# A two-layer hybrid backbone on one core: order of query and value projections, placement of query transposes, first fill, sums of squares, and buffers of the second layer's gate

## The chip, the cores and the metric

The kernel runs on one core of one Trainium2 chip. The metric is the device time of one execution in microseconds. Kernels are compared by the median of their runs; beside it one execution of each kernel is profiled.

## The reference

Two layers work on 512 latent tokens (an 8 x 64 grid) and 256 context tokens of width 1024, all in float32. A layer is:

- a modulation vector from `silu(c) @ ada_w` for latent tokens and `silu(c_ctx) @ ada_w` for context tokens (shift, scale and gate, twice);
- a modulated RMS norm and one input projection, whose columns go to three head groups: a Fourier mixer (256 columns), neighbourhood attention (6 heads of 64, with RMS norm of queries and keys, a relative position bias and a window of 8 x 16; latent queries also see all context keys), and gated linear attention (4 heads, key width 48, value width 96, chunks of 64, one scan per direction, latent scans beginning from the context's final state);
- the concatenated results through one output projection, gated and added to the stream;
- a second modulated RMS norm and a SwiGLU feed-forward network (2816 hidden columns), gated and added.

```python
y = jnp.concatenate([y_fn, y_na, y_gla], axis=-1) @ w_out
x = x + g_m * y
x = x + g_f * swiglu(ada_modulate(x, norm_ffn, sh_f, sc_f), ffn_w1, ffn_w3, ffn_w2)
```

The context stream is updated in the first layer only; the second layer needs its keys, values and states, and no context queries. The output is the latent stream.

## The kernel before, in words

**Precision.** A large product is made of three (`mm3`, line 183): each operand is split into a rounded part and a remainder (`split`, 197: a ScalarE copy and a subtraction on VectorE or GpSimd), and high x high, low x high and high x low are added in PSUM. All these matmuls carry line 181, so the trace is read by tile names: `u` is an unnamed tile, `whl` a split weight, `raw` its load, `a`, `b`, `m`, `y` the four kinds of PSUM buffers (3, 2, 2 and 1 of them, one bank each).

**Order.** Instructions are traced in program order; a list planner with a timeline of its own then orders each engine, except where the block is marked `manual_schedule` for PE (attention, output projection, norm), where PE keeps the written order. All loads and stores are issued by SyncE's queue, one behind the other. An issue waits in that queue for its data, or for the space that it writes. `issue_after(last_mm[0])` keeps PE's instructions of the block behind the last matmul traced so far.

**A layer's stages.** (1) Norm and the input projection, in groups of columns (`group`, 560), one tile of 128 tokens after another: linear-attention values, their queries and keys, gates, then the attention's keys (`wg` 2), values (3) and queries (4). Keys and queries go through a head norm (`headnorm`, 704: a ScalarE square, a VectorE reduction, a GpSimd power, two VectorE products), values through one ScalarE copy; all three are stored to a scratch tensor in HBM (732), to be read back in another order. In layer 0 each tile also takes two steps of `ada_steps` (260), in which VectorE multiplies columns of the modulation weights and PE collects them. Linear attention runs in between: `gate(i)`, `decays(i)` and `kvstate(i)` come 2, 4 and 6 ticks behind tile i (622 to 624). They use the pads `glp` and `kend` and the exponentials `ab`, each in two buffers.

(2) After the Fourier projection the scratch is read back (`load_heads`, 879: keys, then queries; biases; values), the linear-attention outputs are transposed (`to_features`), and the Fourier transform runs as a generator (`fourier`, 1032), whose steps are the weights, the features of each tile of 128 columns, and the two products with the DFT tables. After 6 of its steps (layer 1: 3), `stacks_of_heads` (908) transposes keys and queries of the first pair of heads on PE (924), and splits them into the stacks `st`.

(3) Attention runs over units of a pair of heads and a block of columns (`Heads`, 1150; 5 blocks per pair in layer 0, 4 in layer 1): scores of unit n, transposes of the probabilities of unit n - 1, a fill, and the values of unit n - 1. The fill is work of the output projection's first part (`wo`, over the linear-attention and Fourier features, 5 x 128 rows): a credit in us is raised by 2.4 (layer 1: 2.3) per unit, and products are issued while it is positive:

```python
credit[0] += us
while credit[0] > 0:
    n = next(wo, None)
    if n is None: return
    credit[0] -= n[1] * 3 / 2400
```

The credit begins at -2.4 (1137). What is left of `wo` runs after the last unit.

(4) The second part of the output projection (`wb`, over the attention features) adds into the residual stream (`u<-m,u,u`, line 192 from 994), one product per 128 rows m and stream n: context and latent in layer 0, the two halves of the latent tokens in layer 1. Behind each product `norm_add` (363) squares the new rows on ScalarE (`nsq`) and adds them to `nacc`: stream 0 on VectorE, stream 1 on GpSimd. `norm_sums` (382) sums `nacc` over partitions on PE, with a power on GpSimd; `norm_spread` (397) brings the result back to all partitions (`ndg`); `norm_mod` applies it. At the same time GpSimd splits the first feed-forward weights (1344).

(5) The feed-forward network in three parts; in layer 0 the steps of layer 1's modulation run beside it.

Of the kernel before, what the change touches and what calls it, by code (L numbers as in the profile page):

```python
# [16 lines left out]
F32 = mybir.dt.float32  # L17
F32R = mybir.dt.float32r
U32 = mybir.dt.uint32
AF = mybir.ActivationFunctionType  # L20
ALU = mybir.AluOpType
# [4 lines left out]
KD = 8  # L26
# [116 lines left out]
def hybrid_kernel(tc, d, out, dbg=None):  # L143
    nc = tc.nc
    ctx = ExitStack()
    V, S, G, T = nc.vector, nc.scalar, nc.gpsimd, nc.tensor
# [9 lines left out]
    def mk(p, shape, dt=F32, tag=None, bufs=None):  # L156
        uid[0] += 1
        kw = {}
        if bufs:
            kw["bufs"] = bufs  # L160
        return p.tile(shape, dt, tag=tag or f"u{uid[0]}", name=f"{tag or 'u'}_{uid[0]}", **kw)
# [6 lines left out]
    PA = lambda: mk(psp, [128, 512], F32, "a", 3)  # L168
# [9 lines left out]
    last_mm = [None]  # L178
# [9 lines left out]
    def tt(e, o, a, b, op):  # L188
        e.tensor_tensor(out=o, in0=a, in1=b, op=op)  # L189
# [4 lines left out]
    def act(o, i, f=AF.Identity, **kw):  # L194
        S.activation(out=o, in_=i, func=f, **kw)  # L195
# [164 lines left out]

        return products, finish

    def norm_add(acc, x, k, tp, e):

        if k == 0:
            act(acc, x, AF.Square)
            return
        sq = mk(tp, [128, TL], F32, "nsq", 2)[:, :x.shape[-1]]
        act(sq, x, AF.Square)
        tt(e, acc, acc, sq, ALU.add)  # L370

    def norm_acc(xs, n, tp, e):

# [77 lines left out]
    for l in range(DEPTH):  # L451
        last = l == DEPTH - 1
        ctx_q = not last
# [11 lines left out]
        np0 = pool(nst_, f"n{l}", "left")  # L465
# [81 lines left out]
        tp = pool(p1, f"t{l}", "right")  # L547
# [8 lines left out]
        s1p = pool(s1, f"gs{l}", "left")  # L556
# [3 lines left out]
        def group(src, cols, specs, evac, together=0, w=None, ps=None, after=None):  # L560

            w = w or wgroup(src, cols)
            ps = ps or {}
            for n, (i, c0) in enumerate(specs):
                if n == len(specs) - together:
                    for m, (j, cj) in enumerate(specs[n:]):
                        ps[j] = dense("mbmbya")[:, :cols - cj]  # L570
                    for k in range(KD):
                        for j, cj in specs[n:]:
                            token_major(ps[j], w, j, cj, k)
                if i not in ps:
                    ps[i] = dense("mb" if l == 0 else "mbmby")[:, :cols - c0]
                    for k in range(KD):
                        token_major(ps[i], w, i, c0, k)
                tick()
                evac(i, ps[i])
                next(steps, None)  # L580
                next(steps, None)
                if after:
                    after()
# [42 lines left out]
        both = [(i, 0) for i in tiles]  # L626
        qonly = [(i, 0) for i in qtiles]

        npad = 2
        kend = [mk(s1p, [128, 8, 64]) for _ in range(npad)]  # L630
        glp = [mk(s1p, [128, 8, 64]) for _ in range(npad)]
        qT = {i: mk(gp, [128, 4, 128]) for i in qtiles}
# [9 lines left out]
        def gate(i):  # L642
            zps = PA()[:, :384]
            mm(zps, aT[:, 128 * i:128 * i + 128], alpha, True, True)
            ab = mk(s1p, [128, 512], F32, "ab", 2)[:, :384]
            act(ab, zps, AF.Abs)
            act(ab, ab, AF.Exp, scale=-1.0)
            act(ab, ab, AF.Ln, bias=1.0)
            stt(glp[i % npad][:, :, 0:48], v3(zps), 0.0, v3(ab), ALU.min, ALU.subtract)

        def decays(i):
            gl, ke = glp[i % npad], kend[i % npad]
            heads = lambda a, dp: a[:, 2 * dp:2 * dp + 2].rearrange("p a b -> p (a b)")
            if i not in qtiles:
                dps = PA()
                for dp in range(4):
                    mm(dps[:, 2 * dp:2 * dp + 2], heads(gl, dp), ind, dp == 0, True)
                act(dec[:, i].rearrange("p a b -> p (a b)"), dps[:, 0:8], AF.Exp, scale=1.0 / 16)
            bs = PA()[:, :384]
            for dr in range(2):  # L660
                mm(v3(bs)[:, 4 * dr:4 * dr + 4], tri[:, 2 * dr + 1], gl[:, 4 * dr:4 * dr + 4, 0:48], dr == 0, True)
            ee = mk(s1p, [128, 512], F32, "ab", 2)[:, :384]
            act(ee, bs, AF.Exp, scale=1.0 / 16)
            kb = gqk[i][:, 4:8, 0:48][:, None].to_broadcast([128, 2, 4, 48])
            tt(V, p4(ke), kb, v4(ee), ALU.mult)
            if i in qtiles:
                bi = PA()
                for dp in range(4):
                    mm(bi[:, 128 * dp:128 * dp + 128], heads(gl, dp), tri[:, dp // 2 * 2], dp == 0, True)
                raw = PA()  # L670
                for a in range(4):
                    T.transpose(raw[:, 128 * a:128 * a + 128], heads(gqk[i], a), ident)
                d3 = lambda a: a.rearrange("p (d a b) -> p d a b", d=2, a=2)
                for dst, sgn, x in ((qT[i], 1.0, raw[:, 0:256]), (kT[i], -1.0, raw[:, 256:512])):
                    eb = mk(s1p, [128, 512], F32, "ab", 2)
                    act(eb, bi, AF.Exp, scale=sgn / 16)
                    x = x.rearrange("p (a b) -> p a b", a=2)[:, None].to_broadcast([128, 2, 2, 128])
                    tt(V, dst.rearrange("p (d a) b -> p d a b", d=2), x, d3(eb), ALU.mult)
                    if sgn > 0:
                        for dr in range(2):  # L680
                            G.tensor_copy(dec[:, i, 2 * dr:2 * dr + 2],
                                          d3(eb)[:, dr, :, 63 - 63 * dr::64])
# [137 lines left out]

        group(d["wg"][l, 1], 384, qonly, ev_scr("g"))
        group(d["wg"][l, 2], 384, both, ev_scr("k"), after=between)
        group(d["wg"][l, 3], 384, both, ev_scr("v"), after=between)
        group(d["wg"][l, 4], 384, qonly, ev_scr("q"), after=between)


        ze = [mk(zp, [128, 2, 258], F32R) for _ in range(2)]
# [3 lines left out]
        for m in range(2):  # L831
            sl = slice(128 * m, 128 * m + 128)
            for (hs, n) in ((hc, TC), (hl, TL)):
                if hs is hc and not ctx_q:
                    continue
                ps = dense("mb" if l == 0 else "mbmby")[:, :n]
# [39 lines left out]
        nap = pool(yst, f"nq{l}", "right")  # L876
# [31 lines left out]
        def stacks_of_heads(p):  # L908

            for src, gain in ((kn, None), (qn, qg)):  # L910
                n = 768 if ctx_q or gain is None else 512
                kinds = (0, 1) if gain is None else (2,)
                for hh in range(2):
                    for k in kinds:
                        stacks[0, hh, k] = mk(p, [128, n], F32R, f"st{hh}{k}")
                for (j0, nj) in ((0, 4), (4, 2)):
                    if src is qn and j0 and not ctx_q:
                        continue
                    c0 = 128 * j0 if src is qn else (128 * j0 + 256) % 768
                    sl = slice(c0, c0 + 128 * nj)  # L920
                    pss = [ps()[:, :128 * nj] for ps in (PB, PA)]
                    for j in range(nj):
                        for hh, ps in enumerate(pss):
                            T.transpose(ps[:, 128 * j:128 * j + 128], src[j0 + j][:, 128 * hh:128 * hh + 128], ident)
                    for hh, ps in enumerate(pss):
                        u = [stacks[0, hh, k][:, sl] for k in kinds]
                        if gain is None:
                            split(ps, u[0], u[1])
                        else:
                            act(u[0], ps, AF.Copy, scale=gain)  # L930
                            lo = u[0][64:128]
                            stt(lo, ps[64:128], gain[64:128], lo.bitcast(F32), ALU.mult, ALU.subtract)
# [182 lines left out]
        load_heads(nap, "v", vn)  # L1115
        for _ in range(6 if ctx_q else 3):
            next(fn)
        with tc.issue_after(last_mm[0]):
            stacks_of_heads(nap)
        for _ in fn:  # L1120
            pass
        fst.close()
# [11 lines left out]

        load_streams(range(3))

        credit = [-2.4]

        def fill(us):

# [159 lines left out]
        nst_ = ExitStack()  # L1300
        np0 = pool(nst_, f"fn{l}", "left")
        accs = [mk(np0, [128, TL], F32, "nacc", 2)[:, :st_[1](0).shape[-1]] for st_ in streams]
        engines = (V, G) if ctx_q else (V, G)
        with tc.manual_schedule(engines={mybir.EngineType.PE}):
            since = 0
            for mn, _ in wb:
                if mn is None:
                    continue
                m, n = mn
                norm_add(accs[n], streams[n][1](m), m, np0, engines[n])  # L1310
                if mn == (1, 0):
                    early_w = tc.cur_priority
                if since == (1 if ctx_q else 3):
                    sums = norm_sums((accs[0], accs[0].shape[-1]), np0)
                if since == (2 if ctx_q else 7):
                    rb = norm_spread(sums, np0)
                since += bool(since) or mn == (KD - 1, 0)
# [142 lines left out]
```

## Time and profile before

| | us |
|---|---|
| median of 3 runs | 1687.62 |
| range of the runs | 1684.39 to 2008.04 |
| profiled execution | 1687.75 |
| its span | 1686.0 |
| PE busy in it | 1634.9 |
| VectorE, ScalarE, GpSimd busy | 925.9, 581.4, 236.9 |

The span runs from the first to the last instruction that the profiler shows. PE is TensorE's matmul, PEld its weight load, DVE is VectorE, ACT ScalarE, POOL GpSimd, SP or SPq SyncE's queue, whose entries are issues of transfers. `a <- b` in a list of waits reads "a waited for b"; in a row of an instruction `out<-in` names what it writes and reads. An engine that is busy all the time may still run at a lower clock: PEclk is the granted clock as a share of 2.4 GHz.

### The profile page before, as it was taken

The page shows a single profiled execution, that of the slowest core. Times are in us where ns is not written, and L with a number is a line of the kernel's source. Part 1 is how long each engine was busy: PE and PEld are TensorE (multiplying, and loading weights), DVE is VectorE, ACT ScalarE, POOL GpSimd, SP SyncE. Part 2 cuts the span into 40 slices and gives each one's busy share as a digit, 9 for nine tenths or more (in the row PEclk, how much of TensorE's full clock was granted, in tenths as well). Part 3 has the DMA queues.
Part 4 walks back from the last instruction along what each step waited for, and adds up shares of the span by engine and source line. Part 5 has one row for each costly group of instructions (what it writes and reads, how often), then busy time and mean ns, then how long its engine had stood idle before and what let it go on. Part 6 is the DMA issues. An engine that isn't in the chain of part 4 may idle for free.

```text
span 1686.0 us, 25086 instructions
## 1 busy us (share of the span) xinstructions
PE 1634.9 (97%) x9938; PEld 1415.1 (84%) x9938; DVE 925.9 (55%) x1680; ACT 581.4 (34%) x1030; POOL 236.9 (14%) x280
## 2 busy tenths in 40 slices
PE   6999999999999999999999999999899999999999
PEld 5888898787888888888888889899777888888887
DVE  6799875677755553454533443453577553344332
ACT  4474224444334311221122324832444432222220
POOL 0243331003212300000000011332102200000000
PEclk9999999999899999999999999999899999999999
DMA  9445535634133352342321311222763143223321
GB/s 339 156 153 166 185 104 170 186 91 133 41 122 124 119 186 96 126 153 85 125 63 55 120 46 40 94 91 73 202 166 111 51 138 100 95 86 107 100 86 52
DMA packets 79906, 199.68 MB, mean 118 GB/s; under 512 B 10344, under 2 KB 21164, under 8 KB 78764
## 3 DMA queue, kind: packets, MB, share of 16 engines
q1 hardware_dynamic: 79788, 198.07, 37.3%
q8 instruction: 78, 1.28, 0.3%
q14 instruction: 40, 0.33, 0.1%
HBM read 174.84 MB, written 14.29 MB: 112 GB/s over the span
## 4 chain that ended last, share of the span: by engine, by line
PE 87%; DMA 5%; DVE 3%; ACT 2%; issue 1%; SPq 1%; POOL 1%; ACTq 0%; DVEq 0%; POOLq 0%
PE a L181 29%; PE m L181 25%; PE b L181 21%; PE y L181 10%; PE b L1223 1%; DMA qn<-scr_q 1%; DVE u L192 1%; DVE whl L189 1%; DMA st<-qt 1%; DMA raw<-in_woa 1%; DMA kn<-scr_k 0%; DMA bias<-in_rpb 0%; DVE nacc L189 0%; DMA raw<-in_wg 0%; ACT ab L195 0%
## 5 line engine op out<-in xcount | busy, mean ns | idle before, releaser
L195 ACT ACTIVATE whl<-raw 128x1024 fp32r<-128x1024 f32 (+7 forms) x222 | 204.8, 928 | 386.3 <-PE a L181 140.0
L181 PE MATMUL m<-u,whl 128*128 128x512 f32 (+1 forms) x1278 | 264.8, 359 | 0.5 <-DVE whl L189 0.5
L189 DVE TENSOR_TENSOR whl<-raw,whl 128x1024 fp32r<-128x1024 f32 (+7 forms) x201 | 223.1, 1112 | 73.7 <-ACT whl L195 73.6
L181 PE MATMUL a<-u,whl 128*128 128x512 f32 (+1 forms) x1299 | 249.0, 348 | 2.9 <-ACT u L195 2.4
L181 PEld LDWEIGHTS m<-u,whl 128*128 128x128 f32 x1278 | 212.7, 192 | 33.8 <-issue 1.2
L181 PEld LDWEIGHTS a<-u,whl 128*128 128x128 f32 x1299 | 210.5, 191 | 34.4 <-ACT u L195 2.8
L181 PE MATMUL b<-u,whl 128*128 128x512 f32 (+1 forms) x915 | 184.9, 352 | 3.1 <-DVE whl L189 1.8
L181 PEld LDWEIGHTS b<-u,whl 128*128 128x128 f32 x915 | 152.2, 193 | 26.7 <-DVE whl L189 2.4
L192 DVE SCALAR_TENSOR_TENSOR adac<-adaw,u,adac 128x512 f32<-128x512 f32 x196 | 154.6, 810 | 35.9 <-DMA adaw<-in_adaw 34.5
L181 PE MATMUL b<-whl,u 128*128 128x384 f32 (+1 forms) x696 | 145.6, 344 | 1.8 <-DVE u L192 1.8
L181 PE MATMUL m<-whl,u 128*128 128x384 f32 (+2 forms) x672 | 139.7, 344 | 1.9 <-ACT u L195 1.9
L181 PEld LDWEIGHTS m<-whl,u 128*128 128x128 f32 x672 | 115.6, 188 | 16.3 <-issue 9.6
L181 PEld LDWEIGHTS b<-whl,u 128*128 128x128 f32 x696 | 121.6, 188 | 8.0 <-issue 3.3
L181 PE MATMUL a<-g,whl 128*128 128x512 f32 (+1 forms) x594 | 126.7, 370 | 0.0
L181 PEld LDWEIGHTS a<-g,whl 128*128 128x128 f32 x594 | 103.9, 189 | 19.4 <-DVE ft L192 0.8
L192 DVE SCALAR_TENSOR_TENSOR ft<-ft,a 128x512 f32<-128x512 f32 (+1 forms) x53 | 30.5, 575 | 99.7 <-ACT ft L195 65.2
L181 PE MATMUL y<-u,whl 128*128 128x512 f32 (+1 forms) x420 | 82.5, 349 | 0.1
L181 PEld LDWEIGHTS y<-u,whl 128*128 128x128 f32 x420 | 68.1, 189 | 12.1 <-issue 1.7
L181 PE MATMUL m<-g,whl 128*128 128x512 f32 (+1 forms) x396 | 77.8, 350 | 0.0
L189 POOL TENSOR_TENSOR nacc<-nacc,nsq 128x256 f32<-128x256 f32 (+1 forms) x21 | 21.0, 1002 | 391.4 <-ACT nsq L195 391.3
L181 PEld LDWEIGHTS m<-g,whl 128*128 128x128 f32 x396 | 64.7, 189 | 9.7
L181 PE MATMUL b<-g,whl 128*128 128x256 f32 (+1 forms) x396 | 72.5, 336 | 0.0
(217 smaller groups left out, 2015.2 us busy)
## 6 DMA issues: line engine op xcount, KB each, us to landing
raw<-in_w SPq DMA_DIRECT2D x104, 512.0 KB
adaw<-in_adaw SPq DMA_DIRECT2D x48, 512.0 KB
adaw<-in_adaw SPq DMA_DIRECT2D x64, 256.0 KB
raw<-in_wg SPq DMA_DIRECT2D x40, 384.0 KB
raw<-in_w SPq DMA_DIRECT2D x32, 448.0 KB
adaw<-in_ada SPq DMA_DIRECT2D x8, 1024.0 KB
st<-kt SPq DMA_DIRECT2D x32, 192.0 KB
raw<-in_woa SPq DMA_DIRECT2D x16, 320.0 KB
```

The costliest lines, as they stand in the source:

```text
L181: last_mm[0] = T.matmul(o, lhsT=l, rhs=r, start=start, stop=stop, skip_group_check=True).ins
L189: e.tensor_tensor(out=o, in0=a, in1=b, op=op)
L192: V.scalar_tensor_tensor(out=o, in0=a, scalar=s, in1=b, op0=op0, op1=op1)
L195: S.activation(out=o, in_=i, func=f, **kw)
L1223: T.transpose(ps[:, 128 * j:128 * j + 128], p[:, 128 * j:128 * j + 128], ident)
```

## The change

The group of attention queries is projected before the group of values. `stacks_of_heads` becomes a generator that stops ahead of the keys and ahead of the queries: keys are transposed where they were, then two more steps of the Fourier generator run, and the queries' transposes are kept behind the last matmul of these. The fill's credit begins at 0. For the norm ahead of the feed-forward network, one PSUM bank holds the running sums of squares of stream 0 (both layers) and of stream 1 (layer 1 only): the first square is written there, VectorE adds each later one there, and the last addition writes `nacc` in SBUF as before. Stream 1 of layer 1 so moves from GpSimd to VectorE; in layer 0 it stays on GpSimd and in SBUF. Layer 1 gets three buffers of `ab`, `kend` and `glp` in place of two.

```diff
-    def norm_add(acc, x, k, tp, e):
-
+    def norm_add(acc, x, k, tp, e, ps=None):
+
+        part = acc if ps is None else ps
         if k == 0:
-            act(acc, x, AF.Square)
+            act(part, x, AF.Square)
             return
         sq = mk(tp, [128, TL], F32, "nsq", 2)[:, :x.shape[-1]]
         act(sq, x, AF.Square)
-        tt(e, acc, acc, sq, ALU.add)
+        tt(e, acc if k == KD - 1 else part, part, sq, ALU.add)
...
-        npad = 2
+        npad = 2 + l
...
-            ab = mk(s1p, [128, 512], F32, "ab", 2)[:, :384]
+            ab = mk(s1p, [128, 512], F32, "ab", 2 + l)[:, :384]
...
-            ee = mk(s1p, [128, 512], F32, "ab", 2)[:, :384]
+            ee = mk(s1p, [128, 512], F32, "ab", 2 + l)[:, :384]
...
-                    eb = mk(s1p, [128, 512], F32, "ab", 2)
+                    eb = mk(s1p, [128, 512], F32, "ab", 2 + l)
...
         group(d["wg"][l, 2], 384, both, ev_scr("k"), after=between)
+        group(d["wg"][l, 4], 384, qonly, ev_scr("q"), after=between)
         group(d["wg"][l, 3], 384, both, ev_scr("v"), after=between)
-        group(d["wg"][l, 4], 384, qonly, ev_scr("q"), after=between)
...
             for src, gain in ((kn, None), (qn, qg)):
+                yield
                 n = 768 if ctx_q or gain is None else 512
...
+        first = stacks_of_heads(nap)
+        next(first)
         with tc.issue_after(last_mm[0]):
-            stacks_of_heads(nap)
+            next(first)
+        for _ in range(2):
+            next(fn)
+        with tc.issue_after(last_mm[0]):
+            for _ in first:
+                pass
         for _ in fn:
             pass
...
-        credit = [-2.4]
+        credit = [0.0]
...
-        engines = (V, G) if ctx_q else (V, G)
+        bank = PA()
+        sums_ps = (bank[:, 0:256], None) if ctx_q else (bank[:, 0:256], bank[:, 256:512])
...
-                norm_add(accs[n], streams[n][1](m), m, np0, engines[n])
+                norm_add(accs[n], streams[n][1](m), m, np0, V if sums_ps[n] is not None else G, sums_ps[n])
```

## Rows read from the trace of the kernel before

**Rows 1.** The profile page: engines' busy time, and the clock line of 40 slices.

```profile
PE 1634.9 (97%) x9938; PEld 1415.1 (84%) x9938; DVE 925.9 (55%) x1680; ACT 581.4 (34%) x1030; POOL 236.9 (14%) x280
...
PEclk9999999999899999999999999999899999999999
```

**Rows 2.** Waits of PE, whole run: us in total, times, longest.

```profile
PE a L181 <- DVE nacc L189: 15.7, 3, 11.5
PE a L924 <- DMA qn<-scr_q: 6.1, 5, 2.6
```

**Rows 3.** Windows: stretch, length, busy of each engine (count), PEclk, DMA share, GB/s.

```profile
192.00:228.00 36.00, 36.00 (x263) 33.47 (x262) 28.27 (x57) 8.20 (x16) 8.01 (x6) 1.00 0.55 172
281.00:313.00 32.00, 26.08 (x156) 22.30 (x154) 18.76 (x44) 14.34 (x34) 1.76 (x6) 0.84 0.62 184
403.00:433.00 30.00, 25.01 (x125) 20.21 (x124) 24.69 (x34) 11.81 (x22) 16.09 (x11) 0.92 0.35 110
433.00:442.00 9.00, 9.00 (x45) 9.00 (x45) 6.33 (x18) 2.72 (x6) 1.20 (x1) 0.51 0.35 117
1086.00:1096.00 10.00, 7.33 (x66) 5.94 (x65) 5.13 (x12) 7.41 (x13) 3.82 (x4) 1.00 0.47 140
1203.00:1229.00 26.00, 20.16 (x72) 14.89 (x72) 14.63 (x35) 10.09 (x25) 1.20 (x4) 0.61 0.58 169
1306.00:1316.00 10.00, 7.67 (x39) 7.47 (x39) 5.90 (x14) 5.96 (x11) 6.64 (x6) 0.66 0.43 143
```

**Rows 4.** Waits of PE at 281-313, layer 0.

```profile
PE a L924 <- DMA qn<-scr_q: 2.6, 2, 1.6
PE b L1223 <- DVE rcl L1201: 1.8, 1, 1.8
PE a L181 <- DVE mx L1191: 1.5, 1, 1.5
```

**Rows 5.** Waits of PE at 1186-1229, layer 1.

```profile
PE a L924 <- DMA qn<-scr_q: 3.5, 3, 2.6
PE a L181 <- DVE st L192: 1.6, 1, 1.6
PE b L1223 <- DVE rcl L1201: 1.0, 1, 1.0
```

**Rows 6.** Waits of SyncE's queue at 262-300, layer 0.

```profile
SPq L426 <- PE m L181: 5.0, 2, 4.7
```

**Rows 7.** Timeline of SyncE's queue, layer 1: start, us, what is issued.

```profile
1187.24 0.35 SPq L732 DMA_DIRECT2D scr_q<-nst  x1
1187.64 2.54 SPq L888 DMA_DIRECT2D kn<-scr_k  x4
```

**Rows 8.** VectorE by form at 228-260: count | busy, mean ns | idle before, releaser.

```profile
L709 DVE TENSOR_REDUCE hss<-hsq 128x6 f32<-128x384 f32 x6 | 3.3, 550 | 2.8 <-ACT hsq L195 2.8
...
L189 DVE TENSOR_TENSOR nst<-b,hrs 128x256 f32<-128x256 f32 x6 | 2.2, 415 | 0.3 <-POOL hrs L189 0.3
```

**Rows 9.** Timeline at the end of layer 1's attention: start, us, instruction.

```profile
1287.87 2.99 PE L181 MATMUL m<-u,whl 128*128 128x512 f32 x12
...
1289.27 0.69 DVE L1229 COPY pT<-b 128x512 f32<-128x512 f32 x1
```

**Rows 10.** VectorE by form at 403-426 (first row) and 1297-1309 (other two).

```profile
L189 DVE TENSOR_TENSOR nacc<-nacc,nsq 128x256 f32<-128x256 f32 x7 | 7.3, 1043 | 3.5 <-ACT nsq L195 3.5
...
L189 DVE TENSOR_TENSOR nacc<-nacc,nsq 128x256 f32<-128x256 f32 x7 | 6.8, 967 | 0.3 <-ACT nsq L195 0.2
...
L192 DVE SCALAR_TENSOR_TENSOR u<-b,u,u 128x256 f32<-128x256 f32 x3 | 1.4, 472 | 0.0
```

**Rows 11.** Waits of PE at 403-433, layer 0's output projection and norm.

```profile
PE b L181 <- DVE whl L189: 1.8, 2, 1.1
```

**Rows 12.** Timeline at layer 1's first sum of squares; in brackets the wait.

```profile
1308.65 0.98 PE L181 MATMUL a<-u,nacc 128*128 128x1 f32 x4 [2.33 <-DVE nacc L189]
```

**Rows 13.** Timeline in layer 1's gates.

```profile
1091.56 0.49 ACT L195 ACTIVATE ab<-a 128x384 f32<-128x384 f32 x1 [1.23 <-POOL u L681]
```

## The prediction

> **What bounds the kernel now.** I read the page first: TensorE (PE) is busy 1634.9 of 1686.0 us, so it is the bound nearly everywhere, and no other engine comes near [rows 1]. A change that takes no matmul away can only return two things: the 51 us in which PE stands, and the time in which its clock is at the lower level. The page's clock line is at its top but in slices 11 and 29 of 40 [rows 1]. Second came the waits of PE over the whole run [rows 2]: the largest, 15.7 us for the sums of squares, is mostly one wait of 11.5 us; it lies in the first projection, which calls the norm in its old form, so it stays. Third came the windows of the stretches that the edits touch [rows 3]; the reader is to see two columns there, PE busy against the length, and PEclk. Lost clock is length x (1 - PEclk): 32 x 0.16 = 5.1 us at 281-313 (layer 0, queries loaded, attention begins), 30 x 0.08 = 2.4 at 403-433 (layer 0, output projection and norm), 26 x 0.39 = 10.1 at 1203-1229 (layer 1, queries, attention begins), 10 x 0.34 = 3.4 at 1306-1316 (layer 1, norm): 21.0 us. Last I read, in each stretch, what ended PE's waits.
>
> **The change part by part.** The sum goes against the profiled execution: 1687.75 us, a span of 1686.0 and 1.75 around it. It stands 0.1 above the median of the three runs, 1687.62.
>
> *Queries ahead of values, later query transposes.* In layer 0 PE waits 2.6 us for query rows [rows 4], in layer 1 3.5 us, and 1.6 more for the split of the transposed queries [rows 5]. In layer 0 the exchange of the groups moves no load: the queue that would issue the key loads stands behind a weight load that waits 4.7 us for PE to free the space [rows 6]. In layer 1 it does: the key loads go out 0.05 us after the issue of the last query store [rows 7], and that store stands behind the head norm; with values last it stands behind a single ScalarE copy. The later transposes work in both layers: two Fourier steps, which PE must do anyway, run while the rows land, and the last step covers the split. The moved transposes issue no DMA of their own. Gain between 0 (the rows come later by as much as PE is ahead) and 2.6 + 5.1 = 7.7 us; I take 7.7, since the steps moved in front are longer than any one of these waits: six one-row products and fifteen others per layer. The value loads now stand behind younger stores, but they are issued after keys, queries and bias, and nothing asks for them until the first values.
>
> *What the exchange costs VectorE.* In layer 0 the six query tiles move into the stretch of the ada columns, 192-228, where VectorE is busy 28.3 of 36 us [rows 3]. A tile's head norm is a reduction of 0.55 us and two products of 0.42 [rows 8], so 6 x 1.39 = 8.3 us come in; 7.7 are free. The 0.6 left over is hidden by the four PSUM buffers in which tiles wait: cost 0, and up to 8.3 if the cover fails, because PE's small products of the ada columns stand in order behind VectorE.
>
> *Early fill.* With the credit at 0, the first unit gets 2.4 us (layer 1: 2.3) of output-projection work between its scores and its transposes. There PE now waits 1.5 us for the score buffers and 1.8 for the softmax in layer 0 [rows 4], and 1.0 in layer 1 [rows 5]. Gain 0 to 4.3; taken 4.3, since the weights and the linear-attention part of the inputs are split before. The same work is missing at the end. Layer 1 has 40 x 0.64 = 25.6 us of it for twelve fills of 2.3, so the twelfth is empty: the twelve matmuls of 2.99 us that now run while VectorE copies the last transposes [rows 9] are gone. PE then waits for that copy, which ends at 1289.96, 2.1 us after the matmuls now begin, and somewhat again for the last softmax; 0 to 3.0, taken 2.5. In layer 0 only the leftover after the last values goes, and products whose inputs are ready stand next: 0.
>
> *Sums of squares in PSUM.* Fourteen additions are concerned, seven per layer, on VectorE now and reading SBUF twice. They take 1043 and 967 ns in the mean [rows 10]. The nearest row with one operand in PSUM, the residual update of the same width, takes 472 ns beside the same GpSimd work [rows 10]. No row shows VectorE writing PSUM. Price between 0.47 and today's 1.04; taken 0.47: 7 x 0.57 = 4.0 us of VectorE saved in layer 0, 3.5 in layer 1, where 7 x 0.47 = 3.3 come in for the second half, off GpSimd. On PE's path lie the waits for split weights in layer 0, of which I count the 1.8 us of one row [rows 11], and the 2.3 us for the first sum in layer 1 [rows 12]. Gain 0 to 4.1, taken 4.1. The bank occupies one of three "a" buffers until its last addition; what asks for a buffer then waits for that addition anyway: 0, at worst another 2.3. Late next are the modulation chains after each norm, which stay.
>
> *Third buffer of layer 1.* ScalarE waits 1.23 us for GpSimd to let go of an exponential before it can begin the next gate [rows 13], and PE waits behind that gate (the stretch 1086-1096 holds 2.7 us of PE idle [rows 3]). Gain 0 to 2.7; taken 1.2, ScalarE's row, as the chain behind it is not shortened. The added pads cost two small fills of GpSimd per kind: 0.
>
> *The clock.* The slow clock (1.2 of 2.4 GHz) fills part of the very stretches in which PE waits. I take half of 21.0, 10.5 us. What speaks for all of it: of the five stretches in [rows 3] where PE stands, four have lost clock. What speaks against: 1086-1096 has 2.7 us of idle at full clock, and at 433-442 PE is busy 9.00 of 9.00 us and the clock is still at 0.51 [rows 3]; there matmuls are short and the modulation sets the pace. The Trainium skill, page "TensorE: Matmul & The Clock Gate", section "HAM oscillation — how this bites in real kernels", says that gaps in the matmul work bring the slow clock back and that work without gaps keeps the fast one. By that rule the whole 21.0 would return, as in the first rival; the rows of 433-442 and 1086-1096 do not bear it out.
>
> Sum: 7.7 + 4.3 + 4.1 + 1.2 - 2.5 = 14.8 of waits, 10.5 of clock, 25.3 in all: 1687.75 - 25.3 = 1662.4 us.
>
> **The rivals.**
> - The whole clock returns: 14.8 + 21.0 = 35.8, 1652 us. For it: waits and slow clock share four stretches. Against it: 433-442, and the one-row and one-column products that remain in all of them.
> - The query rows stay late: transfers set their pace, the list planner puts other work in front, and the exchange does nothing, so 7.7 and all clock are missing: 14.8 - 7.7 = 7.1, 1681 us. For it: keys and queries are loaded back to back, at a DMA share of 0.62 and 0.58 in both stretches [rows 3]. Against it: PE has work of its own to put there.
> - VectorE runs out of room at 192-228 (the slower side): PE waits out all 8.3 us of head norms in front of its ada products and runs as long at half the clock, 16.6 us, while the clock elsewhere does not return: -14.8 + 16.6 = +1.8, 1690 us. It decides as soon as PE shows idle time in 192-254; today it has none in 192-228 with VectorE at 0.79 [rows 3].
>
> **How the numbers follow.** Forecast (1654 to 1673, from nearly all of the clock to none, 1687.75 - 14.8 = 1673) 0.55; whole clock or more 0.18; late rows 0.23; slower 0.04. Its own range widened by the bounds of the end of layer 1 and the gate, and reaching to the two nearer rivals without their outer halves, is 1648 to 1681. A difference of 2%, about what a measurement of this kernel can tell from no change, is 33.8 us: under 1653.9 or over 1721.4. Only the first rival is under: 0.18. Over 1721 I give 0.01, as the slower rival ends at 1690. Within: 0.81.
>
> **What would show it.** Right: no wait of PE for query rows in either layer; VectorE additions near 0.47 us with PSUM in their names and no 2.3 us wait before the first sum of layer 1; no wait for the softmax at the first unit; a new wait of some 2 us near the end of attention in layer 1; PEclk near 1.0 where it was 0.61 and 0.66. Wrong: PE idle in the projections of layer 0; additions over 1 us; key loads of layer 1 no earlier relative to the last projection; the clock low in the same stretches although PE no longer waits.

## The result and the profile after

The changed kernel took 1666.07 us in the median of four runs (1664.8 to 1667.3), the kernel before 1686.68 beside it. The ratio is 0.9882, 95% interval 0.9863 to 0.9902: 1.2% faster, so within 2%. Five more runs on another chip gave 1665.8 and 0.9889 (0.9869 to 0.9908). The profiled execution took 1665.79 us, a span of 1663.9.

First the page of the changed kernel. The clock line has no slice under 9 any more, where slices 11 and 29 had 8 [rows 1].

```profile
PE 1616.8 (97%) x9938; PEld 1401.1 (84%) x9938; DVE 919.0 (55%) x1687; ACT 581.1 (35%) x1030; POOL 232.5 (14%) x275
PEclk9999999999999999999999999999999999999999
```

Between the two profiled executions, span minus TensorE's busy time went from 1686.0 - 1634.9 = 51.1 us to 1663.9 - 1616.8 = 47.1: **the waits gave back 4.0 us. The busy time of the same work fell by 18.1 us**: its instructions got shorter, because they ran at the higher clock.

This split holds for these two executions only. The profiled execution of the kernel before had a mean granted clock of 0.984; its 51 executions beside the experiments had 0.986 to 0.992, 0.9889 in the mean. The nine executions of the changed kernel had 0.993 to 0.997, 0.9956 in the mean, and the profiled one 0.997. By these means, lost clock (span x (1 - mean clock)) fell from 18.7 to 7.4 us. Idle time in a slow stretch counts in it, so **at most 11 of the 19 us are clock, and some 8 are not.**

Windows of the changed kernel (columns as in [rows 3], to which they answer):

```profile
190.00:254.00 64.00, 64.00 (x485) 59.04 (x485) 45.26 (x107) 13.37 (x28) 20.40 (x16) 1.00 0.41 136
283.00:313.00 30.00, 23.97 (x156) 20.38 (x155) 17.81 (x43) 13.45 (x33) 1.75 (x6) 0.94 0.67 193
429.60:438.60 9.00, 9.00 (x56) 9.00 (x56) 7.10 (x19) 3.29 (x7) 1.19 (x1) 0.68 0.34 117
1186.00:1229.00 43.00, 38.66 (x262) 32.14 (x261) 32.67 (x74) 22.89 (x52) 2.53 (x12) 1.00 0.78 212
1280.00:1306.00 26.00, 24.11 (x198) 23.51 (x197) 21.23 (x54) 14.48 (x29) 10.89 (x6) 1.00 0.44 150
```

In layer 1's windows no clock is lost; before, 1203-1229 stood at 0.61 and 1306-1316 at 0.66 [rows 3], and the window of layer 1's heads read

```profile
1186.00:1229.00 43.00, 36.38 (x168) 28.86 (x167) 24.35 (x54) 18.32 (x43) 2.76 (x11) 0.76 0.61 168
```

In layer 0's norm a slow stretch remains: the work of 433-442 before (0.51 [rows 3]) now runs at 429.6-438.6, at 0.68. The first scores of layer 1 show what the clock means, before (first fence) and after (start, us, instruction; in brackets the wait in front):

```profile
1217.63 2.08 PE L181 MATMUL a<-st,st 128*128 128x512 f32 x4 [1.57 <-DVE st L192]
```

```profile
1205.10 1.19 PE L181 MATMUL a<-st,st 128*128 128x512 f32 x4 [2.83 <-DVE st L192]
1206.13 2.90 PE L181 MATMUL m<-u,whl 128*128 128x512 f32 x12
```

The same four matmuls take 2.08 us before and 1.19 after, although the wait in front of them has grown from 1.57 to 2.83 us. By stage, from first instructions of each kind in the two timelines (us; the differences sum to the 22.1 of the span):

| stage | before | after | difference |
|---|---|---|---|
| start to layer 0's first key transposes | 281.37 | 282.68 | +1.3 |
| to layer 0's first scores | 18.37 | 15.53 | -2.8 |
| to its last scores | 84.86 | 86.82 | +2.0 |
| to the spread of its norm's factors | 44.69 | 40.86 | -3.8 |
| to layer 1's first norm | 561.66 | 560.29 | -1.4 |
| to layer 1's first key transposes | 208.88 | 207.19 | -1.7 |
| to layer 1's first scores | 17.80 | 11.73 | -6.1 |
| to its last scores | 68.23 | 64.47 | -3.8 |
| to the spread of its norm's factors | 30.69 | 23.59 | -7.1 |
| to the end | 369.45 | 370.74 | +1.3 |

The waits of the changed kernel over the whole run (columns as in [rows 2]): the query rows are gone. Behind the sum of squares stand a new wait of the softmax's transposes and a longer one for the queries' split (2.8 us, before 1.6 [rows 5]).

```profile
PE a L181 <- DVE nacc L189: 14.2, 2, 12.3
PE b L1232 <- DVE p L1211: 4.5, 2, 4.0
```

The wait of 4.0 us lies in layer 0's first unit, where the early fill works. VectorE, SyncE's queue and TensorE there, of the changed kernel:

```profile
298.81 0.33 SPq L1141 DMA_DIRECT2D u<-in_cxt  x1
...
306.50 0.48 DVE L192 SCALAR_TENSOR_TENSOR u<-m,u,u 128x256 f32<-128x256 f32 x1 [1.97 <-DMA u<-in_cxt]
306.90 0.15 DVE L1210 RECIPROCAL rcl<-sml 128x1 f32<-128x1 f32 x1
...
308.10 0.66 PE L1232 MATMUL b<-u,p 128*128 128x128 f32 x4 [4.01 <-DVE p L1211]
```

The early fill reaches the end of an output chunk, whose residual update waits for a stream row that was issued 7.7 us earlier; the softmax's reciprocal stands behind that update in VectorE's order.

### The profile page after: what moved, and what is told of

The parts are those of the page before. It is cut to its first block, busy times and chain, and to the rows that moved or that the text cites. A ratio compares the mean times of both kernels' runs of the same rounds, so it can differ in the third digit from the quotient of the medians.

```text
span 1663.9 us, 25085 instructions
## 1 busy us (share of the span) xinstructions
PE 1616.8 (97%) x9938; PEld 1401.1 (84%) x9938; DVE 919.0 (55%) x1687; ACT 581.1 (35%) x1030; POOL 232.5 (14%) x275
## 5 line engine op out<-in xcount | busy, mean ns | idle before, releaser
L181 PEld LDWEIGHTS a<-g,whl 128*128 128x128 f32 x594 | 103.9, 189 | 19.4 <-DVE ft L192 0.8
L189 POOL TENSOR_TENSOR nacc<-nacc,nsq 128x512 f32<-128x512 f32 (+1 forms) x14 | 15.4, 1098 | 385.9 <-ACT nsq L195 385.9
```

Source lines behind the costliest of these rows:

```text
L181: last_mm[0] = T.matmul(o, lhsT=l, rhs=r, start=start, stop=stop, skip_group_check=True).ins
```

## The experiments

Two theories. **Clock**: the parts shortened TensorE's idle time in the stretches that ran slow, and most of the gain is the clock that came back. **Waits**: each part gave the wait that it removed, and the clock is a matter of its own. Ratios are of times to the kernel before; the changed kernel has 0.9882 and 0.9889.

### One part taken back

**Queries as before.**

```diff
-group(wg[4], 384, qonly, ev_scr("q"), after=between)
 group(wg[3], 384, both, ev_scr("v"), after=between)
+group(wg[4], 384, qonly, ev_scr("q"), after=between)
...
-first = stacks_of_heads(nap)      # keys, two Fourier steps, queries
...
+with tc.issue_after(last_mm[0]):
+    stacks_of_heads(nap)
```

> The changed kernel with its query part taken back: values projected before queries again, all of the heads' transposes in one place. Theory (the gain is clock that came back, and the query part brought back most of it): layer 1's heads wait for the query rows again (about 5 us for the queries' rows and the last split) and run at a granted clock near 0.76 again (10 us), layer 0's heads at 0.83 instead of 0.94 (3 us): 1676 to 1684 us. Rival (the clock came back by another part, the query part gave only its waits): the clock of layer 1's heads stays at 1.00, and the time is 1668 to 1671 us.

1673.85 us, 0.9927 (0.9911 to 0.9943), between the two ranges. The clock of layer 1's heads fell, but to 0.88 and not to 0.76.

```profile
1186.00:1229.00 43.00, 38.56 (x226) 31.46 (x225) 28.41 (x63) 20.78 (x48) 2.11 (x10) 0.88 0.69 194
```

**Fill as before.**

```diff
-credit = [0.0]
+credit = [-2.4]
```

> The changed kernel with the credit of the fill at -2.4 again, so that the first unit of attention in each layer gets none. Theory (in layer 0 the early fill ends in a residual update that waits for a stream row, and the softmax stands behind it in VectorE's queue: 4.5 us of waits there against 3.3 before; in layer 1 it saves about 0.4 us): 1664 to 1667 us, with the 4.0 us wait of layer 0's first unit gone and the two waits of 1.5 and 1.8 us back. Rival (the early fill is what keeps layer 1's clock up): the clock of layer 1's heads falls towards 0.76, and the time is 1670 to 1678 us.

1669.71 us, 0.9901 (0.9887 to 0.9915): 2 to 3 us, on the edge of what can be told, and between the two ranges. The clock of layer 1's heads fell to 0.92, as the rival has it. But the two-buffer run below has the same 0.92 with the early fill in place, so that the fill holds this clock is not shown.

```profile
1186.00:1229.00 43.00, 38.48 (x248) 31.76 (x247) 30.91 (x71) 22.59 (x53) 3.19 (x14) 0.92 0.75 207
```

**Sums as before.**

```diff
-norm_add(accs[n], ..., m, np0, V if sums_ps[n] is not None else G, sums_ps[n])
+norm_add(accs[n], ..., m, np0, engines[n])      # engines = (V, G)
```

> The changed kernel with the sums of squares in SBUF again, the second one on GpSimd in layer 1 too. Theory (the waits and the clock that they cost): additions of about 1.0 us again, the wait for the first sum in layer 1 back (2.3 us) and the clock after it at 0.82 (3.4 us), the last two parts of layer 0's second output half a few us later with the clock near 0.65 after it (3 to 4 us): 1672 to 1678 us. Rival (only the waits): 1668 to 1671 us with the clock as in the changed kernel.

1670.22 us, 0.9918 (0.9896 to 0.9940), under the range of the first theory and in the rival's (one of its six executions took 1681.28 us and weighs in the ratio). Layer 1's wait is back (2.34 us, 2.33 before; first fence, TensorE; second, VectorE by form at 1270-1300; third, the window), yet the clock there stays at 0.93 and is 1.00 after it, and layer 0 has that of the changed kernel (0.93 at 395-445). The wait is this part's; of clock, 26 x 0.07 = 1.8 us went there, where 3.4 were expected.

```profile
1291.93 0.61 PE L181 MATMUL a<-u,nacc 128*128 128x1 f32 x4 [2.34 <-DVE nacc L189]
```

```profile
L189 DVE TENSOR_TENSOR nacc<-nacc,nsq 128x256 f32<-128x256 f32 x7 | 6.8, 969 | 0.3 <-ACT nsq L195 0.2
```

```profile
1280.00:1306.00 26.00, 22.12 (x165) 21.20 (x164) 22.02 (x41) 14.80 (x29) 17.80 (x13) 0.93 0.48 161
```

**Two buffers.**

```diff
-npad = 2 + l
+npad = 2
...
-ab = mk(s1p, [128, 512], F32, "ab", 2 + l)      # three places
+ab = mk(s1p, [128, 512], F32, "ab", 2)
```

> The changed kernel with two buffers again for the second layer's exponentials and pads. Both theories: the wait at the first gates of layer 1 is 2.7 instead of 1.3 us, and the time is 1666.5 to 1668.5 us; a clock that falls after this wait would add up to 6 us (1670 to 1674 us).

1668.83 us, 0.9898 (0.9877 to 0.9919): not to be told from the changed kernel by its time. Its wait at the gates (first row) is 2.22 us, against 1.27 in the changed kernel and 2.67 before. In layer 1's heads, which this edit leaves alone, its clock is 0.92 against 1.00. The wait for the queries' split there is the same to the hundredth, and so are the three in front of it (0.23, 0.31 and 0.37 us in both kernels), but the work behind it runs slowly (other two rows):

```profile
1088.36 0.92 PE L181 MATMUL a<-u,u 128*128 128x192 f32 x4 [2.22 <-DVE u L192]
...
1206.42 2.08 PE L181 MATMUL a<-st,st 128*128 128x512 f32 x4 [2.83 <-DVE st L192]
1208.29 4.72 PE L181 MATMUL m<-u,whl 128*128 128x512 f32 x12
```

In the changed kernel the same rows took 1.19 and 2.90 us. **The same waits went with either clock**, so one profiled execution cannot tell whether 0.92 in place of 1.00 comes from an edit.

### One part alone, on the kernel before

**Only the queries.**

```diff
+group(wg[4], 384, qonly, ev_scr("q"), after=between)
 group(wg[3], 384, both, ev_scr("v"), after=between)
-group(wg[4], 384, qonly, ev_scr("q"), after=between)
...
-with tc.issue_after(last_mm[0]):
-    stacks_of_heads(nap)
+first = stacks_of_heads(nap)      # keys, two Fourier steps, queries
...
```

> The kernel before with the query part alone (queries projected ahead of values, later query transposes). Theory (it is the gaps at the heads of layer 1 that cost the clock there): the wait for the queries' rows goes (6.1 us in both layers), the clock of layer 1's heads rises from 0.76 towards 0.9 to 1.0: 1670 to 1677 us. Rival (the parts share one gain, and this one alone gives what its undoing cost, 7.8 us): 1678 to 1680 us with the clock still under 0.88.

1673.68 us, 0.9933 (0.9919 to 0.9946): this part alone gives 0.67%, some 11 us of the 19 to 20. The clock of layer 1's heads is 0.96, so the theory holds and the rival falls.

```profile
1186.00:1229.00 43.00, 36.66 (x243) 30.00 (x241) 30.53 (x69) 21.93 (x51) 2.54 (x11) 0.96 0.75 209
```

**Only the exchange.**

```diff
+group(wg[4], 384, qonly, ev_scr("q"), after=between)
 group(wg[3], 384, both, ev_scr("v"), after=between)
-group(wg[4], 384, qonly, ev_scr("q"), after=between)
```

> The kernel before with the two projection groups exchanged and nothing else. Theory (the earlier rows are what counts, the later place of the transposes little): layer 1's waits for the query rows go and most of the clock there comes back: 1672 to 1679 us, within 2 us of the whole query part. Rival (the transposes' place is what counts, since the planner still puts them into the rows' way): the waits for the query rows stay above 3 us in all and the time is 1682 to 1687 us.

1679.61 us, 0.9973 (0.9959 to 0.9986): 4.5 us, less than half of the part. That is just over the first theory's range, and the waits stay above 3 us, as the rival has it, but not its time. The waits for query rows over the whole run are

```profile
PE a L924 <- DMA qn<-scr_q: 4.0, 5, 1.3
```

2.9 us of them in layer 0, where the exchange alone changes nothing, and 1.1 instead of 3.5 in layer 1. The rest needs the later transposes. The executions of this kernel also show the clock by themselves (five of the twelve; time in us, mean clock):

```
1675.14 0.995   1677.40 0.993   1679.88 0.991   1681.10 0.990   1685.01 0.989
```

Of the twelve, the fastest and the slowest differ by 9.9 us, and the clock by 0.006, which is 10 us of 1680. The clock is not all of it: another execution at 0.989 took 1681.17 us.

**Only the sums.**

```diff
-norm_add(accs[n], ..., m, np0, engines[n])      # engines = (V, G)
+norm_add(accs[n], ..., m, np0, V if sums_ps[n] is not None else G, sums_ps[n])
```

> The kernel before with the sums of squares in PSUM alone. Theory (waits and the clock after them): the 2.3 us wait of layer 1 and about 2 us of waits in layer 0 go, with 3 us of clock behind each: 1676 to 1681 us. Rival (only the waits): 1682 to 1684 us, with layer 0's stretch after the second output half at the same clock as before.

1681.22 us, 0.9972 (0.9961 to 0.9983): 4.7 us, between the two. In layer 1 the wait is gone and no clock is lost behind it (1280 to 1325 at 1.00). In layer 0 (before in the first row, this run in the second) the clock of 395-445 is 0.93 against 0.86, but TensorE is busy 45.02 us of the 50 against 45.01: no wait went there. Nor is that clock shown to be this part's: the run with dummy work, whose edit is in layer 1 alone, has 0.93 there too (last row). Over its twelve executions the mean clock is 0.9893, against 0.9889 before, so most of these 4.7 us are not clock, which speaks for the rival.

```profile
395.00:445.00 50.00, 45.01 (x236) 39.13 (x236) 37.72 (x62) 21.51 (x39) 21.34 (x13) 0.86 0.36 115
395.00:445.00 50.00, 45.02 (x263) 39.79 (x262) 37.03 (x65) 22.80 (x42) 21.22 (x13) 0.93 0.37 119
1306.00:1325.00 19.00, 17.07 (x141) 16.65 (x141) 13.98 (x35) 8.21 (x18) 1.54 (x3) 1.00 0.31 96
...
395.00:445.00 50.00, 44.96 (x253) 38.09 (x253) 38.12 (x63) 21.77 (x40) 21.36 (x13) 0.93 0.37 120
```

### Idle time filled with dummy work

```diff
+if l and src is qn:
+    for _ in range(16):
+        T.transpose(pss[1][:, :128], ident, ident)
 for j in range(nj): ...          # the transposes of the query rows
...
+if l and not self.pr and not b:
+    with tc.issue_after(last_tr[0]):
+        for _ in range(10):
+            T.transpose(sps[0][:, :128], ident, ident)
 for hh, sp in enumerate(sps): ...   # the scores
```

> The kernel before with dummy transposes of the identity put into two gaps of layer 1's heads: 16 ahead of the first transposes of the queries' rows (the 2.57 us wait) and 10 ahead of the first scores (the 1.57 us wait); they write a PSUM tile that is written again behind them, so nothing that is computed changes. The rows and the splits come no earlier. Theory (TensorE's idle time there takes the clock): the dummies stand in the gaps, the work after them runs at about 1.0 instead of 0.76, and the time falls by 5 to 10 us, to 1676 to 1681 us, although no wait of the data is shorter. Rival (the clock falls for another reason, such as which work runs there, and idle time costs only itself): the clock stays near 0.76 and the time is 1685 to 1690 us.

1681.15 us, 0.9983 (0.9971 to 0.9995): 3 us faster than the kernel before, with 26 instructions more. The window of layer 1's heads in this run, then in the run with only the sums, which leaves these heads as they were; and this run's timeline:

```profile
1186.00:1229.00 43.00, 37.32 (x221) 31.48 (x221) 25.46 (x58) 18.67 (x45) 3.26 (x11) 0.92 0.60 173
...
1186.00:1229.00 43.00, 35.00 (x177) 28.02 (x177) 23.92 (x54) 17.66 (x42) 2.04 (x8) 0.80 0.64 168
```

```profile
1201.61 1.91 PE L924 MATMUL a<-u 128*128 128x128 f32 x16
...
1209.79 0.30 PE L927 MATMUL a<-u,qn 128*128 128x128 f32 x1 [2.25 <-DMA qn<-scr_q]
...
1215.02 2.34 PE L1171 MATMUL a<-u 128*128 128x128 f32 x10
```

The clock rises from 0.76 (0.80 in the run with only the sums) to 0.92: idle time takes it, as the first theory says. The rows did not land quite as before: the second and third end their waits at 1205.66 and 1207.00 instead of 1206.92 and 1208.58, so these two came sooner. In this execution 0.16 x 43 = 6.9 us of clock came back. Over the twelve executions it is less: the mean clock rose from 0.9889 to 0.9909, 3.4 us of lost clock, and the time fell by 3.

The time is just over the range, so the theory's size was wrong. Two things in this trace eat up clock. Where TensorE got faster it arrived at the fourth row earlier and waited 2.25 us there (before, it came at 1210.13 and did not wait), and ten of the dummies ran at the lower clock and took 2.34 us for a gap of 1.57. In this trace **clock given back in front of late data turned into waiting**; how much that is over all executions is not measured.

### The early fill's new wait

The changed kernel ran again beside three variants.

> The changed kernel again, unchanged, beside its variants on one chip. All theories: 1664 to 1668 us.

1665.8 us, 0.9889. In its profiled execution the stream row was issued 0.8 us ahead of the first scores (296.63) instead of 0.6 behind them (298.21), and the wait of the first unit is half of that above, so the price of the early fill in layer 0 changes from run to run:

```profile
295.85 0.33 SPq L1141 DMA_DIRECT2D u<-in_cxt  x1
...
304.55 0.66 PE L1232 MATMUL b<-u,p 128*128 128x128 f32 x4 [2.04 <-DVE p L1211]
```

**Early fill in layer 1 alone.**

```diff
-credit = [0.0]
+credit = [0.0 if l else -2.4]
```

> The changed kernel with the early fill in layer 1 alone (credit -2.4 in layer 0, 0 in layer 1). Undoing it in both layers cost 3.6 us. Theory (the early fill gained in layer 1 alone, where it keeps the clock of the heads at 1.00 against 0.92, and in layer 0 it only exchanges a wait of 3.3 us for one of 4.5): within 1 us of the changed kernel or up to 2 us faster. Rival (it gains in layer 0 too, since 3.4 us of filling are done in the gap): 2 to 4 us slower than the changed kernel.

1667.51 us, 0.9900 (0.9882 to 0.9918). That is 1.7 us slower than the changed kernel beside it, less than the intervals: neither theory is settled. Without fill the first unit waits 2.72 + 1.68 us for its softmax:

```profile
302.71 0.73 PE L181 MATMUL a<-st,st 128*128 128x512 f32 x2 [2.72 <-DVE mx L1200]
305.13 2.25 PE L1232 MATMUL b<-u,p 128*128 128x128 f32 x8 [1.68 <-DVE p L1211]
```

**Half a portion in layer 0.**

```diff
-credit = [0.0]
+credit = [0.0 if l else -1.2]
```

> The changed kernel with credit -1.2 in layer 0: the first unit there gets 12 matmuls, and the residual update at the end of their chunk comes in the second unit, behind the softmax in VectorE's queue. Theory (the 4.0 us wait of the first unit is the softmax standing behind an update that waits for its stream row): that wait falls to 2 to 3 us, and the time by 0.5 to 2 us against the changed kernel. Rival (the wait is the softmax chain's own length): 4 us of waits stay in the first unit and the time does not fall.

1664.3 us, 0.9882 (0.9861 to 0.9903): 1.5 us faster than the changed kernel beside it, not told apart either. The residual update now follows the softmax in VectorE's order; with 0.5 us more the unit waits 3.5 us, against 4.5 in the changed kernel's first execution and 2.5 in its second:

```profile
301.04 0.73 PE L181 MATMUL a<-st,st 128*128 128x512 f32 x2 [1.30 <-DVE mx L1200]
303.45 0.66 PE L1232 MATMUL b<-u,p 128*128 128x128 f32 x4 [1.69 <-DVE p L1211]
```

**The same and one portion more ahead of layer 1's first scores.**

```diff
 pr, b = units[n]
+if l and not n:
+    fill(2.3)
 pairs[pr].scores(b)
```

> As the run before, and in layer 1 one more portion of fill, ahead of the first scores, where TensorE waits 2.83 us for the queries' split behind VectorE's Fourier additions. Theory: this wait goes (covered by 12 matmuls of 2.9 us), the end of layer 1's attention lacks one more portion and gives 0 to 1.5 us back: 1 to 4 us faster than the changed kernel, 1662 to 1665 us. Rival (the fill is as much missed at the end as it covers at the start): equal to the run before.

1670.62 us, 0.9921 (0.9904 to 0.9938): slower by 6 us than the run before. Both expectations fall.

```profile
1198.47 3.01 PE L181 MATMUL m<-u,whl 128*128 128x512 f32 x12
1201.57 1.21 PE L181 MATMUL a<-st,st 128*128 128x512 f32 x4
...
1208.86 0.63 PE L1232 MATMUL b<-u,p 128*128 128x128 f32 x4 [1.94 <-DVE rcl L1210]
1210.74 1.09 PE L1232 MATMUL b<-u,p 128*128 128x128 f32 x4 [1.26 <-DVE kt L189]
1211.48 4.19 PE L181 MATMUL m<-u,whl 128*128 128x512 f32 x9
...
1230.41 1.35 PE L181 MATMUL a<-st,st 128*128 128x512 f32 x4 [1.52 <-DMA st<-qt]
```

The 2.83 us wait is covered as meant. But with 24 matmuls the first unit now reaches the end of a chunk, as the early fill does in layer 0. In VectorE's order:

```profile
1204.39 0.75 DVE L192 SCALAR_TENSOR_TENSOR u<-m,u,u 128x512 f32<-128x512 f32 x1 [0.72 <-DMA u<-xs]
1207.29 0.83 DVE L189 TENSOR_TENSOR whl<-raw,whl 128x640 fp32r<-128x640 f32 x1 [2.15 <-ACT whl L195]
1208.03 0.15 DVE L1210 RECIPROCAL rcl<-sml 128x1 f32<-128x1 f32 x1
```

The update waits for its stream row; the split of the next chunk's weights waits 2.15 us for ScalarE, whose half of it began at 1206.52 after 5.07 us without work; and on both engines the softmax stands behind that split (its exponential at 1207.16, its reciprocal at 1208.03). So 1.94 + 1.26 us of wait come back two steps later, the clock falls behind them (nine matmuls in 4.19 us, later 2.31), and the rows of the next head pair are late too (1.52 us).

## Why the prediction was right, and where only its sum was

The forecast of 1662.4 is 3.7 us under the measured median, and the change lies within 2%, as forecast. Its two halves are not right. Between profiled executions, **14.8 us of waits were forecast and 4.0 came (8.0 in the second profiled execution: 1660.4 - 1617.3 = 43.1 us idle); 10.5 us of clock were forecast and 18.1 came (17.6).** The errors offset each other.

By the mean clock of all executions the clock term was about right (at most 11 us came), and the term that was too large is the waits: some 8 us that are not clock, against 14.8. That the sum came so close is in part luck. It starts from 1687.75, an execution at a clock of 0.984, while the later medians of the kernel before are 1684.0 to 1686.5; from 1685 the same sum would have ended 6 us too low.

- **Queries: the mechanism was right, and it is the largest part** (11 us alone, at most 9 of them clock). No wait for query rows is left in either layer. But of the 7.7 us of waits some came back in two places: TensorE waits 1.38 us for key rows in layer 0 (not in the second profiled execution), and 2.83 us, before 1.57, for the queries' split in layer 1, which stands behind the Fourier additions in VectorE's order. The prediction said that the last Fourier step "covers the split"; that sentence failed, since this step is also what VectorE has in front of it.

```profile
1202.80 0.69 DVE L189 TENSOR_TENSOR u<-raw,u 128x512 fp32r<-128x512 f32 x1 [0.71 <-ACT u L195]
1203.51 0.75 DVE L189 TENSOR_TENSOR raw<-pe,m 128x255 f32<-128x255 f32 x2
1204.29 0.76 DVE L192 SCALAR_TENSOR_TENSOR st<-b,qg,st 64x512 fp32r<-64x512 f32 x1
```

  That the exchange in layer 0 moves no load is borne out by the exchange alone: the key loads still go out 1.1 us after the issue of that weight load (273.06 and 274.16 us; before 270.83 and 271.93), and 2.9 us of waits for query rows stay there.
- **VectorE at 192-228: cost 0, as said.** TensorE is busy 64.00 us of 64 in 190-254; the slower rival is false.
- **Early fill: wrong in layer 0.** Forecast was a gain of 3.3 us; the first unit waits 4.5 us where it waited 3.3, or 2.5 in the second execution. Beside the changed kernel without fill there (2.72 + 1.68 = 4.4 us) it saves between nothing and 1.9. The reason given ("the weights and ... inputs are split before") leaves out what the fill writes: its residual row was not there. In layer 1 the wait fell from 1.0 to 0.6. The 2.5 us that were to be paid back at the end of layer 1's attention are 0.3:

```profile
1272.13 1.56 PE L181 MATMUL y<-pT,vn 128*64 128x128 f32 x16 [0.31 <-ACT pT L195]
```

  The last transposes and the next projection's twelve matmuls stand behind these values and cover VectorE's copy.
- **Sums of squares: the price was right** (taken 0.47 us, measured as below, by VectorE's forms at 395-430 with both operands' names), **and layer 1's 2.3 us went as said.** In layer 0 the 1.8 us did not: TensorE waits 1.5 us for a split weight at another place, and in 395-445 in all no less than before (50 - 44.32 = 5.7 us idle, before 5.0).

```profile
L189 DVE TENSOR_TENSOR a<-a,nsq 128x256 f32<-128x256 f32 x6 | 2.6, 428 | 2.3 <-ACT nsq L195 2.3
...
L189 DVE TENSOR_TENSOR nacc<-a,nsq 128x256 f32<-128x256 f32 x1 | 0.4, 424 | 0.5 <-ACT nsq L195 0.5
```

- **Third buffers: 1.2 forecast, the wait fell by 2.67 - 1.27 = 1.4**, of which 2.22 - 1.27 = 0.95 comes back with two buffers. By time it can't be told from nothing.
- **The clock: too small beside the profiled pair, about right beside the means.** Half of 21.0 us was taken. In the profiled execution all of layer 1's came back; in layer 0 less did (0.94 at 283-313, 0.68 at 429.6-438.6). Two rows were held against the whole clock, and neither carries that weight. The stretch 433-442 was read as busy and slow, so that idle time could not be the cause, but it stands right behind an idle one; in the changed kernel too TensorE waits 0.52, 1.26 and 0.57 us at 425-429, and the work behind them runs at the lower clock. The full clock at 1086-1096 was a matter of one execution: with the same two buffers it is 0.87 there in the run with only the sums, and 0.83 in the two-buffer run. And the size itself, length x (1 - PEclk), counts idle time as lost clock: 1203-1229 holds 26 - 20.16 = 5.8 us of it [rows 3]. The rival of the whole clock was thus right for layer 1, and its 1652 us were missed because the waits gave back so little. By the rule of the Trainium skill that the prediction weighed ("TensorE: Matmul & The Clock Gate", "HAM oscillation — how this bites in real kernels": gaps bring the slow clock, work without gaps keeps the fast one) a rise of the clock was to be expected. The dummies agree with it (0.76 to 0.92); the same waits at either clock, in the changed kernel and with two buffers, show that it does not settle a single execution.

Queries, fill, sums and buffers taken back cost 7.1, 2.7, 5.6 and 2.2 us (ratios less 0.9885, the mean of the two, times 1685): 17.6 of 19.4. That is close to a sum. The mean clock of every execution splits it further (gain against the kernel before by the ratios; lost clock as above, and its fall from 18.7; all in us):

| kernel (executions) | mean clock | lost clock | gain | fall of lost clock | rest |
|---|---|---|---|---|---|
| changed (9) | 0.9956 | 7.4 | 19.4 | 11.3 | 8.1 |
| only the queries (5) | 0.9942 | 9.7 | 11.3 | 9.0 | 2.3 |
| only the exchange (12) | 0.9917 | 14.0 | 4.5 | 4.7 | -0.2 |
| only the sums (12) | 0.9893 | 18.1 | 4.7 | 0.6 | 4.1 |
| dummy work (12) | 0.9909 | 15.3 | 2.9 | 3.4 | -0.5 |
| queries as before (6) | 0.9917 | 13.9 | 12.3 | 4.8 | 7.5 |
| fill as before (5) | 0.9938 | 10.3 | 16.7 | 8.4 | 8.3 |
| sums as before (6) | 0.9947 | 8.9 | 13.8 | 9.8 | 4.0 |
| two buffers (6) | 0.9937 | 10.6 | 17.2 | 8.1 | 9.1 |

An entry is good to 1 or 2 us. The clock is mostly the queries' (9.0 alone, 11.3 - 4.8 = 6.5 when taken back), and the rest is half the sums' (4.1 either way). Of these 4.1 the traces show 2.3, layer 1's wait; where the others lie stays open. So the clock theory holds for the queries, and the waits theory for the sums. What the fill and the buffers give, 2 to 3 us, is inside the intervals.

## What to carry to other kernels

Where TensorE is busy nearly all of the span, compare its busy time for the same count of instructions before and after: a difference there is clock, and it can be larger than the waits that a change removes. But look at the mean clock of several executions before one profile is taken for the kernel: here the profiled pair showed 18 us of clock, and the means at most 11. Price the clock of a stretch by the idle time in and just in front of it, and count what fill work writes and what its end asks for as well as what it reads: an update that waits for its row, or a split that waits for its weights, blocks what stands behind it on its engine.

## What was not expected of the hardware

A wait of 2.83 us in layer 1's heads left the granted clock of the stretch at 1.00 in the changed kernel; in the kernel before the longest wait there was shorter, 2.6 us [rows 5], and with the others around it the clock stood at 0.61 [rows 3]. With two buffers the same 2.83 us, with the same waits in front, left the work behind it at the lower clock. So neither the longest wait of a stretch nor all of its waits tell its clock in one execution. And executions of one kernel differ by 10 us, most of which goes with the clock (0.995 to 0.989).
